# Gathering 102 instead of 100 tokens of an expert layer, with an earlier pace of gathers

## The chip, the core and the metric

The kernel runs on one core of a Trainium2 chip. The metric is the device time of one execution in microseconds. TensorE (PE) multiplies matrices; VectorE (DVE), ScalarE (ACT) and GpSimd (POOL) do the rest; SyncE (SP) issues most of the transfers, and 16 DMA engines carry them out. Each engine works through its own queue in order.

## The reference

One decoder layer on 256 tokens of width 2048: two kinds of attention, a layer norm, the PEER layer, a layer norm, and a gated embedding. The change is in the PEER layer. Each token chooses, for each of 8 heads, 16 of 16384 experts; an expert is one row of `u` and one row of `v`:

```python
eidx = jnp.take_along_axis(cidx, sel, axis=-1)      # 8 heads x 16 experts a token
gates = jax.nn.softmax(top, axis=-1)
...
ub = u[eb]                                          # rows of u, one for each choice
vbk = v[eb]
act = jax.nn.gelu(jnp.einsum('thed,td->the', ub, xb))
w = gb * act
return jnp.einsum('the,thed->td', w, vbk)
```

All is float32.

## The kernel before

The PEER layer is computed in two ways, side by side.

**Dense.** For 156 of the tokens the kernel multiplies with all of `u` and all of `v`. There are 128 blocks of 128 experts. `u_block` loads a block of `u` (128 x 2048 floats, 1 MiB, the tile `wf`, five buffers) with SyncE and multiplies it with the tokens' columns (`XF[:, :, NSP:]`, `NDT = T - NSP` = 156 columns): 16 calls of a matmul, each shown as two records in the profile, with N = 156 columns. ScalarE applies the activation and writes the block into `A0`, `A1` or `A2`. `gate_work` then scales these by the gates, with small one-hot products on TensorE (`ps_G`) between the blocks. `v_block` multiplies them with `v`, in two halves of the width (`dh` 0 and 1). The first six blocks of `u` lie in tiles of their own (`early`), loaded while the queries are computed.

**Sparse.** For the other 100 tokens (`NSP`) only the chosen rows are fetched. The tokens are in groups: 64 tokens with 2 partitions each, 32 with 4, and 4 with 32. One gather, an indirect DMA issued by GpSimd, fetches for a group one row for each of 128 partitions (128 x 8 KB, the tile `gb`, four buffers), so a group of n tokens needs n gathers of `u` rows and n of `v` rows, 200 in all. VectorE uses each of them: a product with the tokens' rows `xq` and a sum for `u`, a scaled addition into `y` for `v`. The rows `xq` of the first two groups come from `s_x1`; those of the third are broadcast from `s_xc`, which holds eight copies of each token's row. At the end, one-hot products over partitions bring the sums to their tokens: `natural_out` for the first 96 tokens (`NNAT`), `third_sums` and `third_out` for the third group.

**The order.** The order is written out by a generator, `sparse_work`, that yields after each gather, and by paces: `gathers(n)` adds n to an account and issues a gather for each whole one. It is called after each block: `GQ` = 1.8 after a query, `GU` = 0.60 after each of the first 64 blocks of `u`, `GUG` = 0.75 after the others, `GVG` and `GV` (0.42 and 0.35) after those of `v`. So that gathers go out no earlier than the loads around them, each has a mark: a tiny DMA on SyncE's queue, behind the loads issued so far, for which GpSimd waits with a copy (`pace`) before it issues the gather. The use of a gather stands three gathers behind its issue.

The choice of experts, the selection, runs on VectorE, with GpSimd's help: first for tokens 0 to 127, head by head, during the queries (`topk_heads(0, ...)`), then for tokens 128 to 255 (`topk_heads(1, ...)`, called the second selection here), of which `run(work, 1)` puts one step after each of the first 64 blocks of `u`. Its results are transposed on TensorE (`ps_gT`) and needed from block 64 on, by `gate_work`. A scheduler places what isn't held by `keep`, which keeps the program order.

Of the kernel before, what the change touches and what calls it, by code (L numbers as in the profile page):

```python
# [9 lines left out]
F32 = mybir.dt.float32  # L10
# [9 lines left out]
P = 128  # L20
T = 256
NT = T // P
D = 2048
# [16 lines left out]
SEG1 = 64  # L40
SEG2 = NIA - SEG1

GROUPS = ((0, 64), (64, 32), (96, 4))

NCOPY = 8
NSP = sum(n for _, n in GROUPS)

NNAT = GROUPS[2][0]
NDT = T - NSP
# [2 lines left out]


GQ = 1.8
GU, GUG = 0.60, 0.75
GV, GVG = 0.35, 0.42
GSCALE = 2.0 ** 15
GB = 5

# [103 lines left out]
def build(tc, a, out):  # L163
    nc = tc.nc
# [307 lines left out]
    XF = xfp.tile([P, ND, T], F32, name="XF")  # L472
# [116 lines left out]
    gin = pools.open("gin", "left", bufs=1)  # L589
# [4 lines left out]
    sel, eig, eact, ew = [], [], [], []  # L594
    for i, (_, n) in enumerate(GROUPS):
        sel.append(gin.tile([P, NNAT], F32R, name=f"sel{i}") if i < 2 else
# [6 lines left out]
    tkl = pools.open("tkl", "left", bufs=1)  # L603
    for i in range(len(GROUPS)):
        if i < 2:
# [53 lines left out]
    keep = tc.keep_in_program_order  # L659
# [42 lines left out]
    def gates(t):  # L702
# [12 lines left out]
        if t == 0:  # L715
            nc.vector.tensor_copy(eg[:NSP, 1].bitcast(F32), g[:NSP])
            for i in range(len(GROUPS)):
                slots(i, 1, by_slot(i, 1))
# [5 lines left out]
    def slots(i, w, src):  # L724

        t0, n = GROUPS[i]
        nc.gpsimd.dma_start(eig[i][:, w],
# [58 lines left out]
    ys = [None for _ in GROUPS]  # L786
# [3 lines left out]
    def gathers(n):  # L790

        nonlocal due
        due += n
        while due >= 1:
            due -= 1
            run(sparse, 1)

    def sparse_work():


        xq = []

        def tokens(i):
            t0, n = GROUPS[i]
            xq.append(gin.tile([P, D], F32, name=f"xq{i}", tag=f"xq{i % 2}"))
            src = a["s_x1"][t0:t0 + n]
            if i == 2:
                src, n = a["s_xc"].rearrange("t c d -> (t c) d"), n * NCOPY
            dma = nc.gpsimd.dma_start if i == 2 else load
            dma(xq[i], src[:, None, :].to_broadcast([n, P // n, D]))  # L810

        tokens(0)
        tokens(1)
        made = []

        dots, acts = [], []

        def advance():

            if acts and gated:  # L820
                i, b = acts.pop(0)
                keep(nc.vector.tensor_tensor(ew[i][:, b], ew[i][:, b],
                                             eig[i][:, 1, b].bitcast(F32), op=ALU.mult))
            if dots:
                i, b = dots.pop(0)
                keep(nc.scalar.activation(ew[i][:, b], eact[i][:, b], AF.Gelu_apprx_tanh))
                acts.append((i, b))

        def use(kind, i, j, g):
            if kind == "u_rows":  # L830
                keep(nc.vector.scalar_tensor_tensor(g, g, 1.0, xq[i], op0=ALU.mult, op1=ALU.mult,  # L831
                                                    accum_out=eact[i][:, j:j + 1]))
            elif j == 0:
                if i < 2:
                    ys[i] = gin.tile([P, D], F32, name=f"y{i}", tag=f"xq{i}")
                else:

                    ys[i] = g
                keep(nc.vector.tensor_scalar(ys[i], g, ew[i][:, j:j + 1], None, op0=ALU.mult))
            else:  # L840
                keep(nc.vector.scalar_tensor_tensor(ys[i], g, ew[i][:, j:j + 1], ys[i],  # L841
                                                    op0=ALU.mult, op1=ALU.add))
                if (i, j) == (1, GROUPS[1][1] - 1):
                    natural_parts()
            if j % SELB == SELB - 1 or j == GROUPS[i][1] - 1:
                advance()
                if kind == "u_rows":
                    dots.append((i, slice(j - j % SELB, j + 1)))

        for kind in ("u_rows", "v_rows"):  # L850
            for i, (_, n) in enumerate(GROUPS):
                for j in range(n):
                    if kind == "u_rows" and (i, j) == (0, GROUPS[0][1] // 2):
                        t0, n2 = GROUPS[2]
                        keep(nc.gpsimd.dma_start(
                            a["s_xc"], a["s_x1"][t0:t0 + n2, None, :].to_broadcast([n2, NCOPY, D])))
                    if kind == "u_rows" and (i, j) == (1, 2 * NGB):
                        tokens(2)

                    mark = gin.tile([1, 1], F32, name="mark", tag="mark", bufs=32)  # L860
                    keep(nc.sync.dma_start(mark, a["c_iota"][0:1, 0:1]))
                    keep(nc.gpsimd.tensor_copy(pace, mark))  # L862
                    g = gin.tile([P, D], F32, name="gb", tag="gb", bufs=NGB)
                    keep(nc.gpsimd.indirect_dma_start(  # L864
                        out=g, out_offset=None, in_=a[kind],
                        in_offset=bass.IndirectOffsetOnAxis(ap=eig[i][:, 0, j:j + 1], axis=0)))
                    made.append((kind, i, j, g))
                    if len(made) >= NGB:
                        use(*made.pop(0))
                    yield  # L870
        while made:
            use(*made.pop(0))
# [22 lines left out]
    def third_sums(ps, d0, d1):  # L895

        for d in range(d0, d1):
            keep(nc.tensor.matmul(ps[:, d * 32:(d + 1) * 32], ys[2][:, d * P:(d + 1) * P], sel[2],
                                  start=True, stop=True))

    def third_out(ps):
        t0, n = GROUPS[2]
        dst = XF[:, :, t0:t0 + n]
        keep(nc.vector.scalar_tensor_tensor(
            dst, dst, ALPHA, ps.rearrange("p (j t) -> p j t", j=ND)[:, :, :n],
            op0=ALU.mult, op1=ALU.add))
# [58 lines left out]
    def run(work, n):  # L965

        for _ in range(n):
            if next(work, "end") == "end":
                return True
        return False  # L970
# [14 lines left out]
    work = topk_work()  # L985
# [22 lines left out]
    for ia in range(SEG1):  # L1008
        if ia == EARLY:
            pools.close("earlyp")  # L1010
            a1p = pools.open("a1p", "right", bufs=1)
            A1 = a1p.tile([P, SEG1 - SEG0, NDT], F32, name="A1")
            iaT, ibT = (a1p.tile([P, T], F16, name=nm) for nm in ("iaT", "ibT"))
            ghf, glf = (a1p.tile([P, T], F32, name=nm) for nm in ("ghf", "glf"))
        u_block(ia, W_of(ia))
        run(work, 1)
        gathers(GU)
    while not run(work, 1):
        pass
    pools.close("tk", "tkl")  # L1020
# [3 lines left out]
    work = gate_work(ohp, (A0, A1), 0, SEG1, GB)  # L1024
# [43 lines left out]
    work = gate_work(ohp, (A2,), SEG1, SEG2, GB)  # L1068
# [248 lines left out]
    ps = ln2_T(0, 0, 2)  # L1317
# [17 lines left out]
    ps = ln2_T(1, 0, 4)  # L1335
# [8 lines left out]
    ps = ln2_T(1, 4, 4)  # L1344
# [8 lines left out]
    ps = ln2_T(0, 8, 4)  # L1353
# [7 lines left out]
    ps = ln2_T(0, 12, 4)  # L1361
# [4 lines left out]
    for d0, k0, k1 in ((8, 12, 14), (12, 14, 16)):  # L1366
        ps = ln2_T(1, d0, 4)
# [42 lines left out]
def _constants():  # L1410
    pos = np.arange(T, dtype=np.float32)
    inv = np.float32(ROPE_THETA) ** (-np.arange(0, ROT, 2, dtype=np.float32) / np.float32(ROT))
    ang = (pos[:, None] * inv[None, :].astype(np.float32)).astype(np.float32)
    cos, sin = np.cos(ang).T, np.sin(ang).T
    h = ROT // 2
    C = np.ones((P, T), np.float32)
    S = np.zeros((P, T), np.float32)
    for s in (0, 64):
        C[s:s + h] = cos
        C[s + h:s + 2 * h] = cos  # L1420
        S[s:s + h] = -sin
        S[s + h:s + 2 * h] = sin
    r = np.arange(P)
    valid = (r[:, None] < r[None, :]).astype(np.float32)
    svalid = np.concatenate([valid, np.ones((P, P), np.float32), valid], axis=1)
    sneg = np.where(svalid > 0, np.float32(0), np.float32(NEG)).astype(np.float32)
    dm = np.where(r[None, :] <= r[:, None], np.float32(0), np.float32(NEG)).astype(np.float32)
    return {
        "c_ropeC": C, "c_ropeS": S, 
        "c_svalid": svalid, "c_sneg": sneg,  # L1430
        "c_dmask": np.concatenate([np.zeros((P, P), np.float32), dm], axis=1),
        "c_tri": (r[:, None] >= r[None, :]).astype(np.float32),
        "c_ones": np.ones((P, P), np.float32),
        "c_ident": np.eye(P, dtype=np.float32),
        **{f"c_sel{i}": (t0 % NNAT + np.arange(P)[:, None] // (P // n)
                         == np.arange(32 if i == 2 else NNAT)[None, :]).astype(np.float32)
           for i, (t0, n) in enumerate(GROUPS)},
        "c_iota": np.broadcast_to(np.arange(P, dtype=np.float32), (P, P)).copy(),
    }
# [71 lines left out]
```

## Time and profile before

| | us |
|---|---|
| median of 3 runs | 1777.39 (1775.11 to 1777.73) |
| the profiled execution's own time | 1776.11 |
| its span in the profile | 1774.2 |
| queries | 414 to 533 |
| dense product with u | 533 to 1093 |
| dense product with v | 1093 to 1665 |

The page lists busy times, the span in 40 slices of 44.4 us, the DMA queues (q1 is SyncE's, q0 GpSimd's with the gathers), the chain of waits that ended last and the costliest groups. In a group's row stand the count, the busy time, the mean of one and the idle time before it with its releaser. A row of the windows has, behind the stretch, the busy time and the count of PE, PEld (weight loads), DVE, ACT and POOL, then TensorE's granted clock, the busy share of the DMA engines and the rate in GB/s. A row of the timeline or the chain begins with the start and the duration. Matmuls overlap, so the time of one is read from a long unbroken piece of the chain, not from its own duration.

### The profile page before, as it was taken

Reading aid. Unit: us, or ns where it says so; the run is one execution under the profiler, and the core shown is the slowest. Engines: PE = TensorE matmul, PEld = TensorE weight load, DVE = VectorE, ACT = ScalarE, POOL = GpSimd, SP = SyncE. Lnnn points to the kernel's source line nnn. Section 1 sums busy time; section 2 is a strip of 40 time slices with the busy share of each in tenths; the row PEclk is TensorE's granted clock in tenths of the full one; section 3 lists DMA queues with packets and bytes.
Section 4 is the critical chain, followed back from the end, with each engine's and each line's share of the span. In section 5 each row is a group of like instructions: output and inputs, shape, how many; then the busy total and the mean of one; then the engine's idle time right before and its main releaser. Section 6 shows DMA issues by size and latency. Waiting matters only on the chain.

```text
span 1774.2 us, 30337 instructions
## 1 busy us (share of the span) xinstructions
PE 1752.7 (99%) x12074; PEld 1647.6 (93%) x12074; DVE 1058.7 (60%) x1699; ACT 540.3 (30%) x1347; POOL 516.4 (29%) x554
## 2 busy tenths in 40 slices
PE   8999999999999999999999999999999999999997
PEld 6888888888889999999999999999999999999786
DVE  5565588664699877345655644876343433344686
ACT  5677468742110100104333313651000000000452
POOL 0143033105346227323333333333223232321000
PEclk9999999999999999999999999999999999999998
DMA  7544644576998999999999999999999999999671
GB/s 284 193 158 163 232 159 145 178 270 219 381 419 309 421 416 417 421 421 420 420 421 413 419 419 418 405 420 397 421 421 420 421 421 420 420 420 405 216 267 59
DMA packets 99822, 606.22 MB, mean 342 GB/s; under 512 B 12824, under 2 KB 14544, under 8 KB 35776
## 3 DMA queue, kind: packets, MB, share of 16 engines
q1 hardware_dynamic: 68368, 388.82, 55.4%
q0 software_dynamic: 30160, 213.10, 29.3%
q8 instruction: 95, 1.56, 0.4%
q10 hardware_dynamic: 1152, 2.36, 0.4%
q14 instruction: 47, 0.39, 0.1%
HBM read 598.36 MB, written 6.03 MB: 341 GB/s over the span
## 4 chain that ended last, share of the span: by engine, by line
PE 93%; DMA 4%; DVE 1%; ACT 0%; issue 0%; SPq 0%; POOL 0%; DVEq 0%; ACTq 0%
PE ps_v L1043 30%; PE ps_u L214 29%; PE ps_qk L202 7%; PE ps_q L214 6%; PE ps_qk L204 4%; DMA wf<-peer_u 2%; PE ps_v L222 2%; PE ps_v L223 2%; PE ps_gate L221 2%; PE ps_gate L223 2%; PE ps_gate L222 2%; PE ps_v L221 2%; DMA wf<-peer_v 1%; PE ps_mix L222 1%; PE ps_mix L223 1%; PE ps_mix L221 1%
## 5 line engine op out<-in xcount | busy, mean ns | idle before, releaser
L1043 PE MATMUL ps_v<-A,wf 128*128 128x156 f32 x4096 | 553.0, 297 | 1.2 <-DMA wf<-peer_v 1.1
L1043 PEld LDWEIGHTS ps_v<-A,wf 128*128 128x128 f32 x4096 | 545.0, 190 | 2.7 <-DMA wf<-peer_v 1.9
L214 PE MATMUL ps_u<-XF,wf 128*128 128x156 f32 x3904 | 528.2, 297 | 1.8 <-DMA wf<-peer_u 1.3
L214 PEld LDWEIGHTS ps_u<-XF,wf 128*128 128x128 f32 x3904 | 519.2, 190 | 3.1 <-ACT A L976 2.0
L841 DVE SCALAR_TENSOR_TENSOR y<-gb,ew,y 128x2048 f32<-128x2048 f32 x94 | 220.9, 2350 | 220.9 <-DMA gb<-v_rows,eig 220.7
L831 DVE SCALAR_TENSOR_TENSOR gb<-gb,xq 128x2048 f32<-128x2048 f32 x100 | 231.7, 2321 | 147.2 <-DMA gb<-u_rows,eig 147.1
L115 DVE TENSOR_TENSOR wl<-wf,wh 128x1024 fp32r<-128x1024 f32 (+1 forms) x199 | 212.7, 1090 | 110.5 <-ACT wh L114 98.9
L862 POOL COPY pace<-mark 1x1 f32<-1x1 f32 x200 | 108.2, 541 | 514.6 <-DMA mark<-c_iota 514.2
L114 ACT CAST wh<-wf 128x1024 fp32r<-128x1024 f32 (+1 forms) x199 | 172.1, 892 | 142.2 <-PE ps_yn L887 30.3
L202 PE MATMUL ps_qk<-X,wh 128*128 128x512 f32 x512 | 185.2, 401 | 0.0
L976 ACT ACTIVATE A<-ps_u 128x156 f32<-128x156 f32 x128 | 38.4, 300 | 433.6 <-PE ps_u L214 361.9
L864 POOL DMA_INDIRECT gb<-v_rows,eig x100 | 137.2, 1372 | 90.1 <-DVE y L841 54.7
L864 POOL DMA_INDIRECT gb<-u_rows,eig x100 | 122.1, 1221 | 126.3 <-DVE gb L831 67.2
L204 PE MATMUL ps_qk<-X,wl 128*128 128x256 f32 x512 | 145.7, 285 | 0.0
L929 ACT ACTIVATE hi<-eq,ghf 128x64 f16<-128x64 f16 x312 | 104.8, 336 | 45.1 <-DVE eq L923 42.2
L202 PEld LDWEIGHTS ps_qk<-X,wh 128*128 128x128 f32 x512 | 96.4, 188 | 21.9 <-issue 1.0
L214 PE MATMUL ps_q<-XF,wf 128*128 128x256 f32 x512 | 113.6, 379 | 0.6 <-DVE XF L509 0.6
L1104 ACT COPY x<-ps_y 128x256 f32<-128x256 f32 (+3 forms) x12 | 5.2, 439 | 346.3 <-DVE st L1103 346.1
L214 PEld LDWEIGHTS ps_q<-XF,wf 128*128 128x128 f32 x512 | 95.9, 190 | 13.1 <-DVE XF L509 0.8
L930 ACT ACTIVATE lo<-eq,glf 128x64 f16<-128x64 f16 x312 | 104.4, 335 | 0.0
L204 PEld LDWEIGHTS ps_qk<-X,wl 128*128 128x128 f32 x512 | 96.3, 188 | 2.5 <-issue 1.3
L947 DVE SCALAR_TENSOR_TENSOR A<-ps_G,A 128x30 f32<-128x30 f32 (+2 forms) x96 | 32.5, 368 | 45.0 <-PE ps_G L938 39.5
(261 smaller groups left out, 1801.0 us busy)
## 6 DMA issues: line engine op xcount, KB each, us to landing
wf<-peer_v SPq DMA_DIRECT2D x128, 1024.0 KB
wf<-peer_u SPq DMA_DIRECT2D x122, 1024.0 KB
wf<-w_qk SPq DMA_DIRECT2D x64, 512.0 KB
wf<-w_out SPq DMA_DIRECT2D x32, 512.0 KB
wf<-peer_wq SPq DMA_DIRECT2D x16, 1024.0 KB
wf<-ple_gate SPq DMA_DIRECT2D x16, 1024.0 KB
wf<-w_v SPq DMA_DIRECT2D x31, 512.0 KB
early<-peer_u SPq DMA_DIRECT2D x6, 1024.0 KB
```

The source lines that it names most:

```text
L114: self.order(nc.scalar.copy(wh, src))
L115: self.order(nc.vector.tensor_tensor(wl, src, wh.bitcast(F32), op=ALU.subtract))
L202: nc.tensor.matmul(ps, wh[:, j * P:(j + 1) * P], xt[:, dt, :], start=dt == 0, stop=False)
L204: nc.tensor.matmul(ps[:, :T], wl[:, j * P:(j + 1) * P], xt[:, dt, :T], start=False, stop=dt == ND - 1)
L214: nc.tensor.matmul(ps[:, :T - t0], wf[:, dt * P:(dt + 1) * P], xt[:, dt, t0:], start=dt == 0, stop=dt == ND - 1)
L831: keep(nc.vector.scalar_tensor_tensor(g, g, 1.0, xq[i], op0=ALU.mult, op1=ALU.mult, accum_out=eact[i][:, j:j + 1]))
L841: keep(nc.vector.scalar_tensor_tensor(ys[i], g, ew[i][:, j:j + 1], ys[i], op0=ALU.mult, op1=ALU.add))
L862: keep(nc.gpsimd.tensor_copy(pace, mark))
L864: keep(nc.gpsimd.indirect_dma_start(out=g, out_offset=None, in_=a[kind], in_offset=bass.IndirectOffsetOnAxis(ap=eig[i][:, 0, j:j + 1], axi ...
L929: nc.scalar.mul(hi[:, j, :], eq[:, j, :], ghf[:, t])
L930: nc.scalar.mul(lo[:, j, :], eq[:, j, :], glf[:, t])
L1043: return nc.tensor.matmul(ps[:, (j % 2) * NDT:(j % 2 + 1) * NDT], vf[:, j * P:(j + 1) * P], W_of(ia), start=False, stop=ia == NIA - 1 and ...
```

## The change

Two tokens pass from the dense to the sparse side: a fourth group of 2 tokens with 64 partitions each, so `NSP` is 102 and N is 154. There are 204 gathers. The fourth group is treated like the third: its rows `xq` are broadcast from `s_xc` by a DMA on GpSimd's queue, and its sums are added in `third_sums`, with a matmul call more for each of the 16 column blocks. The third and fourth `y` no longer stay in a buffer of `gb`; they take the buffers of `xq` in turn. The paces change slightly. In the first eight blocks of `u` one gather is issued after each block, and no step of the second selection, which begins with the ninth.

```diff
-GROUPS = ((0, 64), (64, 32), (96, 4))
+GROUPS = ((0, 64), (64, 32), (96, 4), (100, 2))
...
-GU, GUG = 0.60, 0.75
-GV, GVG = 0.35, 0.42
+GU, GUG = 0.63, 0.75
+GV, GVG = 0.345, 0.40
+
+NFAST, GFAST = 8, 1.0
...
-            if i == 2:
-                src, n = a["s_xc"].rearrange("t c d -> (t c) d"), n * NCOPY
-            dma = nc.gpsimd.dma_start if i == 2 else load
+            if i >= 2:
+                c0 = t0 - NNAT
+                src = a["s_xc"][c0:c0 + n].rearrange("t c d -> (t c) d")
+                n *= NCOPY
+            dma = nc.gpsimd.dma_start if i >= 2 else load
...
-                if i < 2:
-                    ys[i] = gin.tile([P, D], F32, name=f"y{i}", tag=f"xq{i}")
-                else:
-
-                    ys[i] = g
+
+                ys[i] = gin.tile([P, D], F32, name=f"y{i}", tag=f"xq{i % 2}")
...
-                        t0, n2 = GROUPS[2]
+                        t0, n2 = NNAT, NSP - NNAT
...
+                    if kind == "u_rows" and (i, j) == (3, 1):
+                        tokens(3)
...
-            keep(nc.tensor.matmul(ps[:, d * 32:(d + 1) * 32], ys[2][:, d * P:(d + 1) * P], sel[2],
-                                  start=True, stop=True))
+            for i in (2, 3):
+                keep(nc.tensor.matmul(ps[:, d * 32:(d + 1) * 32], ys[i][:, d * P:(d + 1) * P],
+                                      sel[i], start=i == 2, stop=i == 3))
...
-        t0, n = GROUPS[2]
-        dst = XF[:, :, t0:t0 + n]
+        n = NSP - NNAT
+        dst = XF[:, :, NNAT:NSP]
...
         u_block(ia, W_of(ia))
-        run(work, 1)
-        gathers(GU)
+        if ia >= NFAST:
+            run(work, 1)
+        gathers(GFAST if ia < NFAST else GU)
...
-            aps["s_xc"] = dram.tile([GROUPS[2][1], NCOPY, D], F32, name="s_xc")
+            aps["s_xc"] = dram.tile([NSP - NNAT, NCOPY, D], F32, name="s_xc")
```

More of the change, by code (lines that the diff above doesn't have):

```diff
@@ L1435, in _constants @@
         **{f"c_sel{i}": (t0 % NNAT + np.arange(P)[:, None] // (P // n)
-                         == np.arange(32 if i == 2 else NNAT)[None, :]).astype(np.float32)
+                         == np.arange(32 if i >= 2 else NNAT)[None, :]).astype(np.float32)
            for i, (t0, n) in enumerate(GROUPS)},
```

## The prediction, on record before the changed kernel ran

> **What bounds the kernel now.** I read the page first: the busy shares, the slices, the costliest groups.
>
> ```profile
> span 1774.2 us, 30337 instructions
> PE 1752.7 (99%) x12074; PEld 1647.6 (93%) x12074; DVE 1058.7 (60%) x1699; ACT 540.3 (30%) x1347; POOL 516.4 (29%) x554
> ...
> DMA  7544644576998999999999999999999999999671
> GB/s 284 193 158 163 232 159 145 178 270 219 381 419 309 421 416 417 421 421 420 420 421 413 419 419 418 405 420 397 421 421 420 421 421 420 420 420 405 216 267 59
> ...
> L1043 PE MATMUL ps_v<-A,wf 128*128 128x156 f32 x4096 | 553.0, 297 | 1.2 <-DMA wf<-peer_v 1.1
> ...
> L214 PE MATMUL ps_u<-XF,wf 128*128 128x156 f32 x3904 | 528.2, 297 | 1.8 <-DMA wf<-peer_u 1.3
> ```
>
> Two resources are full at once. TensorE is busy for 99%, and the dense product over u and v (L214, L1043) is over a thousand us of it, with 3 us of waits. But from slice 13 to slice 35 the DMA row is 9 throughout and the rate sits mostly at 420 or 421 GB/s, whatever stage is running. So I asked for the stretch from 577 us to the end of v by windows, for its DMA traffic, and for a piece of it where both queues have work.
>
> ```profile
> 577.00:1600.00 1023.00, 1021.13 (x8125) 1015.78 (x8124) 557.79 (x708) 197.76 (x769) 335.28 (x360) 1.00 1.01 418
> 1600.00:1645.00 45.00, 43.87 (x330) 43.56 (x329) 17.86 (x14) 3.74 (x7) 7.09 (x8) 1.00 0.97 392
> ```
> ```profile
> DMA packets 61753, 445.13 MB, mean 417 GB/s; under 512 B 7297, under 2 KB 7317, under 8 KB 7589
> ```
> ```profile
> DMA packets 1744, 12.62 MB, mean 421 GB/s; under 512 B 205, under 2 KB 205, under 8 KB 205
> ...
> q0 software_dynamic: 871, 6.34, 51.0%
> q1 hardware_dynamic: 870, 6.24, 49.9%
> ```
>
> The third answer is 585 to 615 us. There the gathers (q0) and the loads of wf (q1) both have a backlog; they split the engines evenly and get 421 GB/s together, no more than the whole stretch runs at. A load of wf is 1.05 MB, and at q1's 6.24 MB in 30 us it takes 5.0 us, while TensorE eats one in 4.24 us (below): a backlog of gathers eats into the lead of the loads. How much lead is there? Five wf buffers mean that a load goes out about 17 us, four blocks, before its use. The mark behind it on the same queue tells when it has landed:
>
> ```profile
> 1379.94 0.33 SPq L104 DMA_DIRECT2D wf<-peer_v  x1
> 1380.36 0.24 SPq L861 DMA_DIRECT2D mark<-c_iota  x1
> ```
> ```profile
> 1388.60 0.18 POOL L862 COPY pace<-mark 1x1 f32<-1x1 f32 x1 [6.51 <-DMA mark<-c_iota]
> ```
>
> The mark of 1380.4 releases GpSimd at 1388.6, so this load, issued at 1379.9, is in after about 8.7 us, and some 8 us are left before TensorE needs it. So TensorE is the bound by a lead of two blocks; the DMA engines have nearly no idle time behind that. Anything that speeds TensorE up has to be paid for in bytes.
>
> **The narrower product.** N falls from 156 to 154 columns. The chain of waits has long unbroken pieces, from which the time of one record follows:
>
> ```profile
> 479.56 6.91 PE ps_q L214 x32
> ...
> 1235.74 279.85 PE ps_v L1043 x2112
> ...
> 1651.67 1.70 PE ps_y L898 x16
> ...
> 1655.22 1.70 PE ps_y L898 x16
> ```
>
> At 256 columns 6.91 / 32 = 215.9 ns, at 156 columns 279.85 / 2112 = 132.5 ns, so 0.834 ns a column. At 32 columns 1.70 / 16 = 106 ns, far above that line (29 ns): there something else sets a floor, and 154 columns at 130.8 ns lie above it.
>
> ```profile
> L214 PE MATMUL ps_u<-XF,early x192: 296/296/298, 533.0 to 558.8; 128*128 128x156 f32 x192
> ```
> ```profile
> L938 PE MATMUL ps_G<-lo,ohb 128*128 128x64 f16 x312 | 27.5, 193 | 0.0
> L937 PE MATMUL ps_G<-hi,ohb 128*128 128x64 f16 x312 | 27.4, 193 | 0.0
> ```
>
> Two columns save 1.67 ns, times 4096 + 3904 + 192 records = 13.7 us. All but the some 330 records ahead of 577 us, so 13.1 us, fall into the stretch. The gate products lose 8 of their 624 records, at most 54.9 / 624 x 8 = 0.7 us; I count 0.5, in the same stretch. Where TensorE would wait for DMA none of this reaches the end.
>
> **The third and fourth sums.** `third_sums` ran 16 calls (32 records) in the tail; now there are 32 calls, 32 records more at 106 ns = 3.4 us. Nothing covers them:
>
> ```profile
> 1645.00:1667.00 22.00, 22.00 (x160) 20.23 (x159) 16.46 (x37) 7.59 (x17) 0.00 (x0) 1.00 0.56 175
> ```
>
> TensorE is busy for all 22.00 us of that window, and the chain goes through both ps_y rows. The 96 narrower v records there give back under 0.2 us. So +3.3.
>
> **The bytes.** Two tokens are two gathers of u rows and two of v rows, 128 rows of 8 KB each: 4.2 MB. `tokens(3)` broadcasts one more tile, 1.05 MB, and the copy into s_xc has 16 more rows, 0.13 MB: 5.4 MB in all. How much of it goes out ahead of 577 us, where engines idle? Between 541 and 563 us they do:
>
> ```profile
> DMA packets 779, 4.71 MB, mean 214 GB/s; under 512 B 189, under 2 KB 209, under 8 KB 209
> ```
> ```profile
> 554.40 0.29 DVE L635 MAX8 TV<-S 128x8 f32<-128x128 f32 x1
> ...
> 555.99 2.27 DVE L831 SCALAR_TENSOR_TENSOR gb<-gb,xq 128x2048 f32<-128x2048 f32 x1
> ...
> 566.56 2.29 DVE L831 SCALAR_TENSOR_TENSOR gb<-gb,xq 128x2048 f32<-128x2048 f32 x1 [1.65 <-DMA gb<-u_rows,eig]
> ...
> 568.77 0.29 DVE L635 MAX8 TV<-S 128x8 f32<-128x128 f32 x1
> ```
>
> The row of 554.40 begins the first head of the second selection, which stays there in the built order of the changed kernel too; what moves is the rest, from behind the 21st use of a gather (568.77) to behind the 29th. Up to 554 VectorE works on the first selection, which nothing changes. From 556 on five uses run already, and the fifth waits for its data, not for VectorE. So ahead of 570 us the deferred selection can win a use or so, and after that the even split of the queues sets the pace. More marks early don't help either: the marks run ahead of the gathers, which wait for buffers. I take 0.6 gathers (1.5 us) and as ends none and four (no idle time left between 541 and 563: 207 GB/s missing x 22 us = 4.6 MB).
>
> So 4.8 MB more go through the stretch: at its 417 GB/s 11.5 us. Against this stand the lead of the loads, 8 us, of which I let 6.5 be used up (a load that lands just in time still makes small waits), and the slower end of the stretch: 45 us at 392 instead of 421 GB/s, 3.1 us. 11.5 - 6.5 - 3.1 = +1.9 us for the end of v, in which TensorE's 13.1 us have gone into waits for wf. Bounds: if the whole difference to 421 were idle time that can be used (445.13 MB / 421 GB/s = 1057.3 of 1068 us), 7.6 us less, -5.7; if nothing is lent at all, +11.5.
>
> The paces themselves go the same way: u's second half keeps 0.75 gathers to a block that now takes TensorE less, and gets two broadcasts instead of one (`xq2` and `xq3`); v's second pace falls from 0.35 to 0.345, 1.4%, and the block by 1.3%. None makes room.
>
> The Trainium skill (DMA: Bandwidth & Descriptors, Specifications) puts the fabric's ceiling at 435 GB/s; by it (435 - 417) / 435 = 4% of the 1068 us would still be free, more than all terms here together, and the sum would be TensorE's alone, 10.9 us less than before. The trace shows 421 GB/s with a backlog on both queues and no more in any slice, so the sum goes by 421.
>
> **What I count at nothing.** Four more uses on VectorE (2.3 us each) and four more gathers on GpSimd: both engines idle long enough in the stretch (557.79 and 335.28 of 1023 us busy). y2 now takes the buffer of y0 and so waits for its splits; VectorE's own eight splits stand ahead of it in any case:
>
> ```profile
> 1610.88 5.07 DVE L115 TENSOR_TENSOR wl<-y,wh 128x512 fp32r<-128x512 f32 x8
> ...
> 1615.87 1.28 DVE L839 TENSOR_SCALAR gb<-gb,ew 128x2048 f32<-128x2048 f32 x1
> ...
> 1633.46 2.35 DVE L841 SCALAR_TENSOR_TENSOR gb<-gb,ew 128x2048 f32<-128x2048 f32 x1 [2.60 <-DMA gb<-v_rows,eig]
> ```
>
> The last use ends at 1635.8, 15.9 us ahead of the first ps_y row; two more uses, the last gather some 5 us later, still fit. `tokens(3)` stands in GpSimd's queue ahead of the last u gather, and its buffer xq1 is free by then. If that cover went, the tail would lose what the last use is late.
>
> **Sum.** +1.9 for the stretch, +3.3 for the tail = +5.2, say +5. The profiled execution took 1776.11 us, so 1781.1; the median of the runs is 1777.39, 1.3 above it, which puts the forecast at 1782.4. About 0.2% (3.6 us) is what a measurement here can tell from no change.
>
> **Rivals.** (1) DMA has room after all, TensorE stays the bound: -13.7 - 0.5 + 3.3 = -10.9, so 1766.5. For it: TensorE waits 2.4 us in all now, and the loads have 8 us in hand. Against it: DMA share 1.01 over 1023 us, with 421 at paces as different as the 585 to 615 piece and v. 0.10. The Trainium skill's ceiling (above) speaks for it.
>
> (2) The first eight blocks do take four gathers, as the move is arranged for: 3.4 more than I count, 8.5 us, 1773.9, half of it within 0.2%. For it: 214 GB/s over 22 us. Against it: the rows of VectorE above. 0.20.
>
> (3) The second selection comes too late. It begins eight blocks later and has to be done by block 61 instead of 53, where TensorE transposes its gates:
>
> ```profile
> L774 PE MATMUL ps_gT<-ident,gate x2: 272/272/273, 761.8 to 761.9; 128*128 128x128 f32 x2
> ```
> ```profile
> 733.24 0.28 DVE L712 TENSOR_REDUCE gs<-gate 128x8 f32<-128x128 f32 x1
> ...
> 735.91 2.29 DVE L831 SCALAR_TENSOR_TENSOR gb<-gb,xq 128x2048 f32<-128x2048 f32 x1 [1.83 <-DMA gb<-u_rows,eig]
> ```
>
> In the built order that reduction stood behind 49 uses and stands behind 59 now. Before, 28 uses after the 21st took 733.2 - 568.8 = 164 us, 5.9 us each. At that rate the 59th comes 38 x 5.9 = 223 us after 568.8, at 792, and block 61 starts at 533 + 61 x 4.19 = 788.6: TensorE would wait 4 us, up to 7 with the transposes that follow, behind which every u block stands. It decides where the gathers' pace is over 5.8 us. DMA catches up meanwhile, so that only part adds to the forecast: 1782.4 + 5 = 1787. 0.25.
>
> **The numbers.** Forecast 0.45, of which two thirds are slower by over 0.2% and a third within. (1) is faster, (2) half and half with a little more within, (3) slower: faster 0.10 + 0.08 = 0.18, same 0.16 + 0.12 = 0.28, slower 0.29 + 0.25 = 0.54. The range leaves out (1) and the far end of (3), and takes in -5.7 and +11.5 for the stretch in part: 1772 to 1790.
>
> **What would show it.** In the changed profile: v and u records at 131 ns in unbroken pieces; waits of TensorE for wf<-peer_u and wf<-peer_v at 8 to 15 us instead of 2.4; the stretch still at 417 to 421 GB/s; ps_y pieces of 3.4 us. I am wrong if those waits stay under 4 us and v ends ten us earlier, or if the stretch runs well above 421 GB/s.

## The result: 1.2% slower, 17 us beyond the forecast

The changed kernel takes 1799.4 us in the median of 4 runs (1797.42 to 1801.16), the kernel before 1777.56 beside it on the same chip: a ratio of 1.0124, 95% interval 1.0105 to 1.0142. The forecast was 1782.4, its range 1772 to 1790. The profiled execution took 1797.65 us.

The page of the changed kernel, with the rows that answer to those of before:

```profile
span 1795.9 us, 30414 instructions
PE 1750.0 (97%) x12098; PEld 1638.1 (91%) x12098; DVE 1066.2 (59%) x1699; ACT 538.6 (30%) x1340; POOL 509.4 (28%) x566
...
DMA  7544644557998999999999999999999999999571
GB/s 281 190 166 163 234 152 146 209 220 271 389 418 306 422 420 407 417 421 420 421 420 414 384 420 421 418 420 395 421 422 420 421 421 420 404 417 408 183 261 62
...
L1048 PE MATMUL ps_v<-A,wf 128*128 128x154 f32 x4096 | 546.8, 295 | 7.1 <-DMA wf<-peer_v 7.1
...
L216 PE MATMUL ps_u<-XF,wf 128*128 128x154 f32 x3904 | 526.3, 295 | 18.8 <-DMA wf<-peer_u 17.4
```

TensorE's share falls from 99% to 97%, and its idle time ahead of L216 grows from 1.8 to 18.8 us, ahead of L1048 from 1.2 to 7.1. The DMA row is 9 as before. What TensorE waits for, in total, times and longest:

```profile
PE ps_u L216 <- DMA wf<-peer_u: 17.4, 30, 3.1
PE ps_v L1048 <- DMA wf<-peer_v: 7.1, 5, 2.9
```

So 24.5 us of waits for loads stand where 2.4 stood, and where 8 to 15 were forecast. To see where the time goes I cut both profiled executions at the first TensorE record of certain blocks (worked out from the records' starts; us):

| kernel | u 0-8 | u 8-64 | u 64-128 | v, first half | v, second half to load 252 | tail of v | rest |
|---|---|---|---|---|---|---|---|
| before | 34.4 | 241.8 | 285.1 | 285.5 | 257.6 | 27.4 | 109.3 |
| after | 33.9 | 251.1 | 293.4 | 281.7 | 257.5 | 35.9 | 109.9 |
| difference | -0.5 | +9.3 | +8.3 | -3.8 | -0.1 | +8.5 | +0.6 |

The tail is the last four loads; the products of the last three of them are held back and done in eight pieces, with the sums over partitions between them. One place gives what the narrower product promised: the first half of v has 2048 records, at 1.67 ns each 3.4 us, and is 3.8 faster. Both halves of u and the tail cost 26.1 us.

**u's blocks 8 to 64.** What the DMA engines moved in this stage, in the kernel before and then in the changed one:

```profile
DMA packets 14113, 101.03 MB, mean 418 GB/s; under 512 B 1766, under 2 KB 1786, under 8 KB 1802
```
```profile
DMA packets 14603, 104.51 MB, mean 416 GB/s; under 512 B 1829, under 2 KB 1851, under 8 KB 1867
```

The 3.5 MB more are 8.4 us at 416 GB/s, of the 9.3 lost. In the trace 67 gathers are issued by block 64, and 63 before. The traffic by queue (packets, MB, share of the 16 engines) between 577 and 650 us, in the same order:

```profile
DMA packets 4397, 30.50 MB, mean 418 GB/s; under 512 B 649, under 2 KB 669, under 8 KB 685
...
q1 hardware_dynamic: 2285, 16.54, 54.9%
q0 software_dynamic: 2105, 13.87, 46.0%
```
```profile
DMA packets 4321, 30.76 MB, mean 421 GB/s; under 512 B 571, under 2 KB 571, under 8 KB 571
...
q1 hardware_dynamic: 2159, 15.60, 51.2%
q0 software_dynamic: 2155, 15.07, 49.7%
```

In these 73 us the engines move as much as before; what changes is who gets it. The gathers, asked for sooner, take 1.2 MB more, and the loads of wf get 0.94 MB less, nine tenths of a block. The Trainium skill (DMA: Bandwidth & Descriptors, Queues, rings and completion order) says that an engine takes turns between the queues that have work, a packet at a time. The trace agrees: with work on both, 2159 and 2155 packets. A block of u then costs what its load takes, as the timeline of the changed kernel shows around 810 us (start, duration, wait in brackets):

```profile
807.61 4.42 PE L216 MATMUL ps_u<-XF,wf 128*128 128x154 f32 x32 [0.54 <-DMA wf<-peer_u]
812.57 4.42 PE L216 MATMUL ps_u<-XF,wf 128*128 128x154 f32 x32 [0.53 <-DMA wf<-peer_u]
817.53 4.42 PE L216 MATMUL ps_u<-XF,wf 128*128 128x154 f32 x32 [0.54 <-DMA wf<-peer_u]
```

From start to start it is 4.96 us, where 32 records of 131 ns are 4.19. The loss is 0.77 us a block and the wait shown is 0.54: a record is shown with 295 ns though the next can follow after 131, so the row of waits understates the loss.

**u's blocks 64 to 128.** One stretch stands out, where `tokens(3)` broadcasts xq3. Windows of after, then of before:

```profile
995.00:1020.00 25.00, 21.89 (x190) 21.63 (x190) 14.10 (x23) 8.62 (x35) 6.10 (x8) 1.00 1.02 355
```
```profile
995.00:1020.00 25.00, 25.00 (x205) 24.90 (x204) 14.85 (x22) 8.98 (x37) 9.56 (x10) 1.00 1.01 419
```

The engines are as busy (1.02), but move 355 instead of 419 GB/s, and TensorE loses 3.1 us at once. The broadcast of xq2, which reads 32 rows of the same tensor four times each, shows no such fall in the changed kernel:

```profile
815.00:831.00 16.00, 15.07 (x127) 14.56 (x126) 10.32 (x12) 9.55 (x41) 3.98 (x6) 1.00 1.01 420
```

Besides, the whole stage moves 121.4 MB instead of 119.3.

**The tail.** TensorE's timeline at the end of v in the changed kernel:

```profile
1657.87 0.79 PE L1048 MATMUL ps_v<-A,wf 128*128 128x154 f32 x4 [2.90 <-DMA wf<-peer_v]
1660.34 1.40 PE L1048 MATMUL ps_v<-A,wf 128*128 128x154 f32 x4 [1.67 <-DMA wf<-peer_v]
...
1661.96 0.63 PE L890 MATMUL ps_yn<-wl,sel 128*96 128x512 f32 x1
1662.38 0.63 PE L890 MATMUL ps_yn<-wh,sel 128*96 128x512 f32 x1
...
1666.20 0.39 PE L890 MATMUL ps_yn<-wh,sel 128*96 128x512 f32 x1
1666.43 0.39 PE L890 MATMUL ps_yn<-wl,sel 128*96 128x512 f32 x1
...
1669.17 3.65 PE L902 MATMUL ps_y<-sel,y 128*128 128x32 f32 x32
...
1674.49 3.65 PE L902 MATMUL ps_y<-sel,y 128*128 128x32 f32 x32
```

Three things are late here. The last loads are waited for: 2.90 and 1.67 us, 4.6 where before had 1.1. Behind these waits TensorE runs slower for some us: four records take 1.40 us instead of 0.79, and a 512-column product follows the next by 0.42 us where 4 us later it is 0.23. And the pieces of 32-column products hold 32 records instead of 16.

### The profile page after: what moved, and what is told of

It is laid out like the page before. It is cut to its first block, busy times and chain, and to the rows that moved or that the text cites. A ratio compares the mean times of both kernels' runs of the same rounds, so it can differ in the third digit from the quotient of the medians.

```text
span 1795.9 us, 30414 instructions
## 1 busy us (share of the span) xinstructions
PE 1750.0 (97%) x12098; PEld 1638.1 (91%) x12098; DVE 1066.2 (59%) x1699; ACT 538.6 (30%) x1340; POOL 509.4 (28%) x566
## 4 chain that ended last, share of the span: by engine, by line
PE 83%; DMA 15%; DVE 1%; ACT 0%; issue 0%; SPq 0%; POOL 0%; DVEq 0%; ACTq 0%
PE ps_v L1048 28%; PE ps_u L216 21%; DMA wf<-peer_u 11%; PE ps_qk L204 7%; PE ps_q L216 6%; PE ps_qk L206 3%; DMA wf<-peer_v 3%; PE ps_v L224 2%; PE ps_gate L223 2%; PE ps_gate L225 2%; PE ps_v L225 2%; PE ps_gate L224 2%; PE ps_v L223 2%; PE ps_mix L224 1%; PE ps_mix L225 1%; PE ps_mix L223 1%
## 5 line engine op out<-in xcount | busy, mean ns | idle before, releaser
L1048 PE MATMUL ps_v<-A,wf 128*128 128x154 f32 x4096 | 546.8, 295 | 7.1 <-DMA wf<-peer_v 7.1
L1048 PEld LDWEIGHTS ps_v<-A,wf 128*128 128x128 f32 x4096 | 538.9, 190 | 9.1 <-DMA wf<-peer_v 8.3
L216 PE MATMUL ps_u<-XF,wf 128*128 128x154 f32 x3904 | 526.3, 295 | 18.8 <-DMA wf<-peer_u 17.4
L216 PEld LDWEIGHTS ps_u<-XF,wf 128*128 128x128 f32 x3904 | 513.3, 190 | 26.4 <-ACT A L980 14.1
L842 DVE SCALAR_TENSOR_TENSOR y<-gb,ew,y 128x2048 f32<-128x2048 f32 x98 | 230.4, 2351 | 235.0 <-DMA gb<-v_rows,eig 234.8
L835 DVE SCALAR_TENSOR_TENSOR gb<-gb,xq 128x2048 f32<-128x2048 f32 x102 | 235.9, 2316 | 162.4 <-DMA gb<-u_rows,eig 162.4
L865 POOL COPY pace<-mark 1x1 f32<-1x1 f32 x204 | 100.3, 492 | 480.7 <-DMA mark<-c_iota 479.8
L980 ACT ACTIVATE A<-ps_u 128x154 f32<-128x154 f32 x128 | 38.3, 299 | 446.4 <-PE ps_u L216 379.5
L216 PE MATMUL ps_q<-XF,wf 128*128 128x256 f32 x512 | 113.6, 379 | 0.6 <-DVE XF L511 0.6
L216 PEld LDWEIGHTS ps_q<-XF,wf 128*128 128x128 f32 x512 | 95.9, 190 | 13.1 <-DVE XF L511 0.8
L951 DVE SCALAR_TENSOR_TENSOR A<-ps_G,A 128x30 f32<-128x30 f32 (+3 forms) x93 | 31.9, 372 | 43.0 <-PE ps_G L942 38.7
```

The costliest lines, as they stand in the source:

```text
L216: nc.tensor.matmul(ps[:, :T - t0], wf[:, dt * P:(dt + 1) * P], xt[:, dt, t0:], start=dt == 0, stop=dt == ND - 1)
L1048: return nc.tensor.matmul(ps[:, (j % 2) * NDT:(j % 2 + 1) * NDT], vf[:, j * P:(j + 1) * P], W_of(ia), start=False, stop=ia == NIA - 1 and ...
```

## The experiments

My theory after the result: DMA is full in every stage, five buffers can't carry work from one stage to another, and so each byte costs its full time, more where it is asked for in a bunch. Rivals: the second selection comes too late; the tail's longer sums; the paces alone.

**Narrow alone**: what is TensorE's gain worth without the bytes? The dense side of the kernel before leaves the last two tokens out.

```diff
-NDT = T - NSP
+TD = T - 2
+NDT = TD - NSP
...
-            nc.tensor.matmul(ps[:, :T - t0], wf[:, dt * P:(dt + 1) * P], xt[:, dt, t0:],
+            tn = TD if t0 else T
+            nc.tensor.matmul(ps[:, :tn - t0], wf[:, dt * P:(dt + 1) * P], xt[:, dt, t0:tn],
...
```

> The kernel before, with 100 gathered tokens, its paces and its bytes, but the dense product over 154 columns: the last two tokens are left out of u, the gates and v. Bytes theory (from 577 us the DMA engines are full, so TensorE's gain goes into waits for wf): at most 4 us faster than before, and TensorE's waits for wf grow from 2.4 us to some 10. Rival, TensorE is the bound and the extra bytes alone cost the time: 13 to 14 us faster, waits under 4 us.

1774.69 us, ratio 0.9989 (0.9979 to 0.9998): 13.7 us of TensorE's time bring 2.4. The waits of TensorE:

```profile
PE ps_v L1045 <- DMA wf<-peer_v: 4.9, 10, 1.7
...
PE ps_u L216 <- DMA wf<-peer_u: 3.5, 9, 0.6
```

8.4 us of waits stand for 2.4 before, with not a byte more. DMA is a bound nearly as tight as TensorE, as the prediction had it.

**Old paces**: all of the change, but the paces and the order of the kernel before.

```diff
-GU, GUG = 0.63, 0.75
-GV, GVG = 0.345, 0.40
+GU, GUG = 0.60, 0.75
+GV, GVG = 0.35, 0.42
...
-NFAST, GFAST = 8, 1.0
+NFAST, GFAST = 0, 1.0
```

> The changed kernel with 102 tokens, but the paces and the order of before (0.60, 0.75, 0.42, 0.35; a step of the second selection after each of u's first 64 blocks, no fast start). Bytes theory: the same 449.8 MB go through the stretch, so 15 to 24 us slower than before, like the change. Rival, the order (the fast start and the late selection flood the queue early): at most 6 us slower than before, and the waits at 617 to 685 us gone.

1802.64 us, 1.014 (1.0123 to 1.0157): no better in all. u 8 to 64 takes 242.9 us, 8.2 less than in the changed kernel, but the tail takes 48.1, 12.2 more. The paces now fall short of 204 gathers and the generator flushes the rest in one go. SyncE's queue, then TensorE's:

```profile
1623.30 0.34 SPq L106 DMA_DIRECT2D wf<-peer_v  x1
1623.73 3.94 SPq L864 DMA_DIRECT2D mark<-c_iota  x4
```
```profile
1655.95 1.40 PE L1048 MATMUL ps_v<-A,wf 128*128 128x154 f32 x4 [7.02 <-DMA wf<-peer_v]
1660.91 1.40 PE L1048 MATMUL ps_v<-A,wf 128*128 128x154 f32 x4 [3.56 <-DMA wf<-peer_v]
```

Four marks in a row let four gathers out beside the last loads, and TensorE waits 7.02 and 3.56 us for these loads. In this run the broadcast of xq3 goes out 18 us later, at 1019.9 us, and the low rate moves with it:

```profile
1020.00:1043.00 23.00, 20.55 (x178) 20.02 (x176) 9.24 (x14) 6.85 (x29) 5.27 (x7) 1.00 1.01 337
```

**New paces**: the kernel before, 100 tokens, with the changed paces, fast start and late selection.

```diff
-GU, GUG = 0.60, 0.75
-GV, GVG = 0.35, 0.42
+GU, GUG = 0.63, 0.75
+GV, GVG = 0.345, 0.40
+
+NFAST, GFAST = 8, 1.0
...
-        run(work, 1)
-        gathers(GU)
+        if ia >= NFAST:
+            run(work, 1)
+        gathers(GFAST if ia < NFAST else GU)
```

> The kernel before with 100 tokens, but the new paces, the fast start and the second selection from the ninth block. Bytes theory: bytes as before, within 4 us of before. Order: 10 to 18 us slower, with waits for wf at 617 to 685 and 777 to 847 us as in the changed kernel.

1785.1 us, 1.0049 (1.0032 to 1.0066): +8 without one byte or column changed, between what the two theories had said. u 8 to 64 takes 250.4 us, nearly all of after's loss there.

**Fewer gathers**: the changed kernel without 16 of its 204 gathers (eight of u, eight of v, of the first group), paces in proportion.

```diff
-        due += n
+        due += n * 188 / 204
...
-                for j in range(n):
+                for j in range(n - 8 if i == 0 else n):
```

> The changed kernel without 16 of its 204 gathers and their uses (8 of 64 slots of the first group, in u and in v; those experts are left out), all paces scaled by 188/204. 16.8 MB less, 40 us of the DMA engines. Bytes theory: TensorE is the bound again and shows its gain, 1764 to 1770 us, waits for wf under 5 us. Order: the waits of the early blocks stay, 1775 us or more.

1779.42 us, 1.0012 (1.0002 to 1.0021). A miss: with less traffic than the kernel before and the narrow product I had expected 1764 to 1770. The profiled execution is the slowest of the ten (1783.44 us; the fastest took 1773.84), so its segments show more loss than the median has. In it v is faster than in any other of these kernels (281.3 and 253.9 us), but u 8 to 64 takes 250.4 us, about as with all gathers, and the tail 34.9. What is saved later does not mend what is late early. But by block 64 this kernel has no more gathers out than the kernel before (63 in both). What it has more is three gathers by block 32 (42 to 39) and the broadcast of xq2, which stands eight gathers earlier in its order and goes out in block 56, not in block 63 as in the changed kernel or 67 as before:

```profile
779.68 0.58 POOL L814 DMA_DIRECT2D xq<-s_xc  x1 [7.46 <-DVE ew L826]
```

Which of the two costs how much of the 8.6 us isn't shown. In the tail it is not the bytes:

```profile
1656.00:1668.00 12.00, 12.00 (x75) 11.97 (x75) 4.52 (x10) 3.40 (x7) 0.00 (x0) 0.72 0.31 104
```

TensorE is busy throughout these 12 us and DMA for a third, yet the granted clock is 0.72.

**Late selection and fast start**: the two halves of the new order, each alone on the kernel before. First the selection from the ninth block:

```diff
-        run(work, 1)
+        if ia >= 8:
+            run(work, 1)
```

> The kernel before (100 tokens, its paces) with one part of the change: the second selection begins with the ninth block of u. Theory, selection: VectorE's selection held the gathers back at 609 to 680 us, which left the wf loads more than half of the engines; moved by eight blocks, gathers and loads split evenly for longer, so blocks 8 to 64 of u take some 6 to 9 us longer and the kernel is 6 to 9 us slower. Rival, fast start: nothing changes (within 3 us).

1778.97 us against 1777.99, 1.0008 (0.9998 to 1.0017): no difference. I had put the +8 on the selection; that fell. Then paces and fast start with the selection where it was:

```diff
-GU, GUG = 0.60, 0.75
-GV, GVG = 0.35, 0.42
+GU, GUG = 0.63, 0.75
+GV, GVG = 0.345, 0.40
+
+NFAST, GFAST = 8, 1.0
...
-        gathers(GU)
+        gathers(GFAST if ia < NFAST else GU)
```

> The kernel before (100 tokens) with the new paces and one gather after each of u's first eight blocks, but the second selection from the first block on, as before. Selection theory: within 3 us of before. Fast start: 6 to 9 us slower, with waits for wf at 617 to 685 us.

1786.09 us, 1.0047 (1.003 to 1.0064), and u 8 to 64 at 253.5 us. The paces and the fast start carry all of the +8, and it is lost in the stage where they bring gathers forward.

**Spread rows**: the changed kernel, with xq3 read from 128 different rows of s_x1 instead of 16 rows eight times each.

```diff
                 n *= NCOPY
+                if i == 3:
+                    src, n = a["s_x1"][:P], P
```

> The changed kernel, but the broadcast of the fourth group's rows xq3 reads 128 different rows of s_x1 instead of 16 rows of s_xc eight times each (the fourth group's sums then come from other tokens' rows). The bytes are the same. Theory, repeated rows: the rate between 995 and 1020 us goes from 355 back to some 415 GB/s, TensorE's 4.4 us of waits there go, and the kernel is 3 to 6 us faster than the changed one. Rival, bytes alone: no faster than the changed one by over 2 us.

1794.95 us, 1.0097 (1.008 to 1.0113): 4.5 below the changed kernel, 4.9 when each is taken against the kernel before on its own chip. The window of the broadcast:

```profile
995.00:1020.00 25.00, 24.55 (x210) 24.18 (x209) 11.65 (x18) 8.75 (x37) 6.27 (x7) 1.00 1.02 421
```

421 GB/s instead of 355, with the same bytes. u 64 to 128 falls from 293.4 to 289.5 us.

**Sums twice**: the kernel before, each product of `third_sums` computed twice.

```diff
-            keep(nc.tensor.matmul(ps[:, d * 32:(d + 1) * 32], ys[2][:, d * P:(d + 1) * P], sel[2],
-                                  start=True, stop=True))
+            for _ in range(2):
+                keep(nc.tensor.matmul(ps[:, d * 32:(d + 1) * 32], ys[2][:, d * P:(d + 1) * P], sel[2],
+                                      start=True, stop=True))
```

> The kernel before, with each product of third_sums done twice, which gives the tail the 32 records more of 32 columns that the change brings, and nothing else. Theory, PE time alone: 3.4 us slower than before. Rival: the longer piece of narrow products also lowers the granted clock behind it, as in the run with fewer gathers (0.72 between 1656 and 1668 us): 5 to 8 us slower, with the clock under 0.9 behind a ps_y piece.

1783.42 us, 1.0036 (1.0023 to 1.0048): +5.4, where 32 records more are 3.4, as the rival had it. The rest is in the clock column, here of this kernel and then of the kernel before:

```profile
1652.00:1662.00 10.00, 10.00 (x85) 10.00 (x85) 5.45 (x12) 2.44 (x5) 0.00 (x0) 0.95 0.38 126
1662.00:1672.00 10.00, 10.00 (x67) 9.44 (x67) 4.61 (x11) 2.83 (x7) 0.00 (x0) 0.88 0.79 203
```
```profile
1652.00:1662.00 10.00, 10.00 (x84) 10.00 (x84) 7.35 (x18) 3.39 (x7) 0.00 (x0) 1.00 0.57 202
1662.00:1672.00 10.00, 9.40 (x52) 6.71 (x51) 6.57 (x21) 5.09 (x14) 2.81 (x5) 1.00 1.01 324
```

TensorE waits for nothing in these 20 us, and is still granted 0.95 and 0.88.

**One sum**: the counterpart, the changed kernel with the third group's products alone (the fourth group's are left out).

```diff
-            for i in (2, 3):
+            for i in (2,):
...
-                                      sel[i], start=i == 2, stop=i == 3))
+                                      sel[i], start=True, stop=True))
```

> The changed kernel, but third_sums takes the third group's products alone (the fourth group's sums are left out), so the tail has 32 records less. Theory, sums and clock: 3.4 us for the records and about 2 us of lower clock behind them, 4 to 7 us faster than the changed kernel, and the granted clock behind the ps_y pieces at 1.00. Rival, records alone: 3 to 4 us faster, with the lower clock in the tail as in the changed kernel.

1795.25 us, 1.01 (1.0081 to 1.0119): 4.2 below the changed kernel, 3.7 when each is taken against the kernel before on its own chip. The records are 3.4 of it; what is left for the clock is too little to tell. The clock is still low, but only behind the waits for the last loads (3.24 and 1.67 us here); between 1670 and 1680 us, with the ps_y pieces, it is 1.00:

```profile
1660.00:1670.00 10.00, 10.00 (x48) 8.32 (x47) 7.67 (x17) 2.48 (x4) 0.00 (x0) 0.74 0.25 80
```

**Early pace**: the kernel before, with five gathers moved from u's second half to its first; bytes, columns and sums as they were.

```diff
-GU, GUG = 0.60, 0.75
+GU, GUG = 0.68, 0.67
```

> The kernel before (100 tokens, 200 gathers, the order of before) with GU = 0.68 in place of 0.60 and GUG = 0.67 in place of 0.75: five gathers move from u's second half into its first, nothing else. Theory, stages: the DMA engines have to deliver in each stage what its pace asks for, and what is done early buys nothing later, since only five loads can be ahead; blocks 8 to 64 take 7 to 12 us longer, the second half at most 2 us less, 6 to 11 us slower in all. Rival, total bytes: within 3 us of before.

1795.81 us, 1.0108 (1.0086 to 1.013): +18.7 from one pair of numbers, where I had expected 6 to 11. u 8 to 64 loses 11.5 us, as the theory has it: five gathers are 5.2 MB, 12.5 us at 420 GB/s. But u 64 to 128 does not give it back; it loses 10.6 more. The engines have less to do there, as expected:

```profile
953.00:1105.00 152.00, 151.44 (x1239) 150.40 (x1239) 73.02 (x101) 42.20 (x171) 48.77 (x48) 1.00 0.99 394
```

394 GB/s, so no bound by DMA; TensorE is busy for 151.44 of the 152 us. Of the 10.6 I find two places: blocks 64 to 72 (41.2 us instead of 35.7) and 120 to 128 (40.0 instead of 35.6). At 842 us the gate products wait for ScalarE, which computes their factors one by one, 0.24 us apart:

```profile
843.14 0.19 PE L937 MATMUL ps_G<-hi,ohb 128*128 128x64 f16 x1 [0.56 <-ACT hi L929]
843.38 0.19 PE L938 MATMUL ps_G<-lo,ohb 128*128 128x64 f16 x1
843.62 0.19 PE L937 MATMUL ps_G<-hi,ohb 128*128 128x64 f16 x1
...
845.32 6.16 PE L214 MATMUL ps_u<-XF,wf 128*128 128x156 f32 x32
```

Elsewhere these records are 0.03 us apart, and a block's 32 u records take 4.24 us from start to start, where these take 6.0. With the last loads of u the same is seen again, at a lower clock:

```profile
1105.00:1115.00 10.00, 9.20 (x50) 7.91 (x49) 5.85 (x8) 8.59 (x38) 2.90 (x5) 0.83 1.01 417
```

In these 10 us ScalarE is busy for 8.59. What puts that work there I did not isolate; that part of the +18.7 stays open.

**Shifted**: 102 tokens, the early order of before, the additional gathers at later paces (enough that none is flushed), spread rows.

```diff
-GU, GUG = 0.63, 0.75
-GV, GVG = 0.345, 0.40
+GU, GUG = 0.60, 0.78
+GV, GVG = 0.36, 0.42
...
-NFAST, GFAST = 8, 1.0
+NFAST, GFAST = 0, 1.0
...
+                if i == 3:
+                    src, n = a["s_x1"][:P], P
```

> 102 tokens with u's first 64 blocks as before (0.60, no fast start, a step of the selection after each), the later paces raised so that the last gather goes out no later (0.78, 0.42, 0.36), and the fourth group's rows read from 128 different rows (as in spread_rows; those sums come from other tokens' rows). Theory, stages: blocks 8 to 64 as before or 1 to 2 us less, the second half of u 5 to 8 us longer, no waits at 777 to 847 us; 8 to 14 us slower than before, so 8 to 13 us faster than the changed kernel. Rival, total bytes: like spread_rows, 17 us slower than before.

1793.86 us, 1.0087 (1.0068 to 1.0106): +16.8, where spread rows has +17.0. That is what the rival had said, the total of the bytes; the theory of stages had 8 to 14. It wins 6.9 us in u 8 to 64 (244.2) and loses it again: v's two halves take 286.5 and 261.4 us instead of 281.7 and 257.0. Wherever the bytes are put, they cost.

**Last earlier**: the changed kernel with v's second pace higher, so that the last gathers are out before the last loads.

```diff
-GV, GVG = 0.345, 0.40
+GV, GVG = 0.36, 0.40
```

> The changed kernel with GV = 0.36 in place of 0.345, so that the last gathers go out some eight half-blocks of v earlier. Theory, last gathers: they no longer share the engines with the last loads of v, TensorE's waits of 4.6 us at 1658 to 1660 go back to the 1.1 us of before, and the kernel is 2 to 4 us faster than the changed one. Rival: v's pace is over what the engines deliver, the waits move ahead into v's blocks, and nothing is won (within 2 us, or slower).

1798.98 us, 1.0118 (1.01 to 1.0137): nothing won, as the rival had it. The tail falls from 35.9 to 31.4 us and TensorE has no long wait there any more, but v's second half rises from 257.5 to 261.7.

None of these is a faster version: narrow alone, the only one below the kernel before, leaves two tokens out.

## Why the prediction was wrong

**Step by step.** *TensorE's saving* was right in size and place: 295 ns and 131 ns a record, and only 2.4 of 13.7 us come through when nothing else changes (narrow alone). *The bytes* were right in size: the stretch from 577 us to the end of v moved

```profile
DMA packets 62406, 449.75 MB, mean 416 GB/s; under 512 B 7385, under 2 KB 7407, under 8 KB 7679
```

in 1081 us, 4.6 MB more than before, for the 4.8 forecast, at about the rate forecast. *The fast start* brought as little ahead of 577 us as I said: 26 gathers are issued between 400 and 577 us in both kernels. *Rival 1* (DMA has room) and *rival 2* (four gathers early) fall with these. *Rival 3*: the gates are transposed late as its condition said, at

```profile
L776 PE MATMUL ps_gT<-ident,gate x2: 272/272/273, 801.9 to 802.0; 128*128 128x128 f32 x2
```

instead of 761.8, but TensorE did not wait for them; it waited for loads ahead of them, and its block 61 was late itself. Late selection alone costs nothing that can be measured.

**The step that failed** is the one that turned +11.5 us of bytes into +1.9: 6.5 us lent from the loads' lead, and 3.1 from the slow end of the stretch. The slow end was there: it filled, from 392 to 421 GB/s.

```profile
1613.00:1658.00 45.00, 42.10 (x322) 41.87 (x321) 19.85 (x16) 3.74 (x7) 10.70 (x12) 1.00 1.01 421
```

The lead was not there to lend. In the kernel before TensorE already waits for loads between 577 and 823 us, and again for the last loads of v, which is where the stretch ends:

```profile
PE ps_u L214 <- DMA wf<-peer_u: 1.3, 3, 0.5
```
```profile
1643.98 0.80 PE L1043 MATMUL ps_v<-A,wf 128*128 128x156 f32 x4 [1.13 <-DMA wf<-peer_v]
```

The same wait ends at 1657.87 us in the changed kernel (above), and with spread rows at

```profile
1653.04 1.17 PE L1050 MATMUL ps_v<-A,wf 128*128 128x154 f32 x4 [2.27 <-DMA wf<-peer_v]
```

Without the lead the prediction's own sum for the end of the stretch is 11.5 - 3.1 = +8.4. In the profiled executions the stretch ends 9.1 later with spread rows, 10.4 with shifted (1654.35 us), and 13.9 in the changed kernel, above even the +11.5 for nothing lent at all; by the run with spread rows, 4.8 of that is the repeated rows. Behind the end of the stretch +3.3 was forecast, and the changed kernel, whose span is 21.7 longer, loses 7.8 there.

Two faults lie in that step. First, I read the lead at one place, 8 us at 1380 us, and treated 1068 us as one account, in which a surplus at one place pays for a lack at another. With five buffers of wf a load can go out four blocks early and no more, and where TensorE waits already, nothing is left. Early pace shows it: its account is that of the kernel before, and u 8 to 64 loses 11.5 us that no later stage gives back. Second, the change itself asks for about five gathers more by block 64 (8 x 1.0 + 56 x 0.63 = 43.3 instead of 64 x 0.60 = 38.4); I saw that the gathers would not go out sooner in the idle engines, and not that they would then stand as a backlog against the loads. I wrote that marks early "don't help"; at 100 tokens they harm, by 8 us (fast start).

**Terms that were mis-sized.** `tokens(3)`: counted by its bytes, 1.05 MB, 2.5 us; reading 16 rows eight times each cost 4.5 to 4.9 us beyond that. That price was in no term and no rival. The tail: the records cost what the prediction says, as the chain of waits of the changed kernel shows,

```profile
1669.33 3.49 PE ps_y L902 x32
...
1674.65 3.49 PE ps_y L902 x32
```

3.6 us more than the two pieces of 1.70. But the tail grew by 8.5: 3.4 more wait for the last loads (2.90 and 1.67 instead of 1.1), and about 2 of lower clock (from the first record behind the first wait to the first ps_y it is 11.3 us, in the kernel before 7.5; 1.67 of the difference is the second wait). These make 9.1; the narrower records give back 0.2, and the other 0.4 I can't place. The prediction has no term for waits or clock in the tail.

**How it adds up.** In the segments, the losses are u 8 to 64 +9.3 (backlog of early gathers; 8 of it at 100 tokens too), u 64 to 128 +8.3 (some 4 the repeated rows, the rest the bytes of the second broadcast and of the gathers), tail +8.5, and against these -4.4 of the narrower product. These are not independent: shifted moved most of the first loss into v and was no faster for it.

The Trainium skill (TensorE: Matmul & The Clock Gate, HAM oscillation) warns of idle gaps over about 3.4 us, behind which matmuls run at half clock. The trace agrees on the rate (0.42 us for 0.23 behind the waits) and not on the threshold: the gaps in the changed kernel's tail are 2.90 and 1.67 us, and in the rows of sums twice there is no wait at all. By which rule the clock falls stays open: fewer gathers ran at 0.72 with TensorE busy throughout and a single wait, of 1.70 us, 11 us earlier; one sum ran at 0.74 behind its waits.

## What to carry to other kernels

When two resources are full together, balance them stage by stage, over a stretch no longer than the buffers reach, and take the lead of the loads as a reserve for jitter, not as time to spend. Moving work from one resource to the other then costs its full price on the second, while little of what the first gains comes through (here 2.4 of 13.7 us). A transfer that reads few rows many times should be priced by a row of its own kind, and a pace that asks for more than the idle engines can take is a backlog against whatever else is queued.

## What the runs showed of the hardware

- A broadcast from 16 rows, each read eight times, pulls all traffic down from 419 to 355 GB/s for 25 us, at a busy share of 1.02; from 128 rows it runs at 421, and from 32 rows, each read four times, at 420.
- Two queues with a backlog share the engines by packets: 2159 to 2155 over 73 us. With both queues at work no stretch quoted here is above 422 GB/s, at any split; long ones that are full stay at 416 to 421.
- The granted clock falls to 0.72 to 0.95 around the tail's small products and behind waits of 2 to 3 us, which costs about 2 us in the changed kernel's tail and in that of sums twice.
